# The modulated input's buffer starts at another offset modulo 1024 bytes

## The chip, the core and the metric

The kernel runs on one core of a Trainium2 chip. The metric is the device time of one execution in microseconds; three executions of the kernel before took 1462.16, 1462.6 and 1463.55 us, median 1462.6.

## What is computed

Two groups of 128 tokens (context and latent) pass through a trunk of two layers. Each layer has three sub-layers, and each of these reads its input after a modulation with a scale and a shift:

```python
h = modulate(x, mod[:, :, 0], mod[:, :, 1])                       # x * (1 + scale) + shift
x = layer_norm(ALPHA * x + 0.5 * mod[:, :, 2] * swiglu(h, w_in, w_out), ...)
m, new_ctx = token_mixer(modulate(x, mod[:, :, 3], mod[:, :, 4]), lp, ctx, rope)
x = layer_norm(ALPHA * x + mod[:, :, 5] * m, ...)
h = modulate(x, mod[:, :, 6], mod[:, :, 7])
x = layer_norm(ALPHA * x + 0.5 * mod[:, :, 8] * swiglu(h, w_in2, w_out2), ...)
```

The model width is 1024, the hidden width of a feed-forward block 2816. The mixer projects its input to convolution, retention, attention and gate columns, works on each, and merges them.

## The kernel before, in words

All 256 tokens go through together, as the columns of matmuls; features lie on the 128 partitions. To keep float32 accuracy, weights and activations are each split into a rounded high part and a remainder ("hi" and "lo"). A product is three matmuls of 256 columns: hi weights with hi input, hi weights with lo input, lo weights with hi input (`mmA`). In every one the weights are the stationary operand (128 x 128 numbers, 512 bytes of each partition) and the input is the moving one (256 numbers, 1024 bytes of each partition).

Weights come in units of 512 KB. Each is loaded into `ring_raw` (4 slots), rounded by ScalarE into `ring_hi`, and its remainder is written by VectorE into `ring_lo` (5 slots each), three units ahead of TensorE. A unit of 8 k-tiles is 24 matmuls.

The modulated input of the current sub-layer stands in `ring_U`, 16 KB of each partition: for each of 8 k-tiles its hi part (1024 bytes) and then its lo part. `build_u` fills it once per sub-layer, six times in all. Its readers are these:

- the gate and up projections of a feed-forward block: 44 units, in four blocks;
- the mixer's projections with 256 columns (`proj(ps, self.u)`): 47 units, in two mixers. So 270 units, or 6480 matmuls, read `ring_U` as the moving operand;
- `bunit` in the mixer, the other way round: there a piece of `ring_U` is stationary and 512 columns of the weights move (`mmB`), 384 matmuls in two mixers.

All other products of split numbers read tenant tiles, called T in the profile's rows (or CM): T1, T2, T3, T4, T6, T7 and CM. They hold hidden activations, the normed latents and the merged branches in the same hi/lo layout, and the same `mmA` or `mmB` reads them.

The buffers are laid out one after the other in the order of `RINGS`. In the kernel before, the byte offsets in each partition are these: `ring_raw` 16512, `ring_hi` 32896, `ring_lo` 53376, `ring_ada` 73856, `ring_U` 90240; then the smaller rings and constants; then T4 164800, T2 181184, T3 189376, T1 197568, T6 205760, CM 213952, T7 222144. Modulo 1024, the weight rings and `ring_U` are at 128, and all seven tenant tiles are at 960. Weight k-tiles advance by 512 bytes, so a stationary tile of weights begins at 128 or 640 modulo 1024. The hi and lo parts of an input advance by 1024.

The order of each engine's instructions is set when the program is built, by a list scheduler with its own cost table (`Program.order`). It knows nothing of addresses. L458 is the one matmul call, L480 and L484 are VectorE's calls, L518 is ScalarE's, L463 the four-strip matmuls of the modulation weights.

Of the kernel before, what the change touches and what calls it, by code (L numbers as in the profile page):

```python
# [8 lines left out]
F32 = mybir.dt.float32  # L9
# [7 lines left out]
P = 128  # L17
# [111 lines left out]
def _units():  # L129
    out = []  # L130
    for l in range(L):
        for seq in (_ffn_units(1), _mix_units(), _ffn_units(2)):
            for key, parts in seq:
                out.append((l, key, parts, sum(len(ks) * len(cols) for _, ks, cols in parts)))
    return out
# [93 lines left out]


N_RAW = 4
N_HL = 5
N_ADA = 4
ROUNDS = [0, 0, 8, 8, 8, 0, 8, 0, 0, 8, 8, 2, 8, 8, 8, 4, 8, 2]
# [26 lines left out]
class Op:  # L261
    __slots__ = ("eng", "dur", "fn", "deps", "succ", "late", "due", "chain", "left", "ready", "nbytes", "pad")

    def __init__(self, eng, dur, fn, chain, due, nbytes, pad):
        self.pad = pad
        self.eng, self.dur, self.fn, self.chain, self.due, self.nbytes = eng, dur, fn, chain, due, nbytes
        self.deps, self.succ = set(), []
        self.late, self.left, self.ready = 1e18, 0, 0.0


class Program:
    """Operations in an order that is right, with what each reads and writes; `order` gives every
    engine its own order, by the latest start that keeps the tensor engine's main chain moving."""

    def __init__(self):
        self.ops, self.writes, self.reads = [], {}, {}
# [18 lines left out]
        return name, p0, p0 + dims[0][1], lo, hi  # L295

    def real(self, ap):
        """The access in the kernel's own tile: a tile that shares its memory with earlier ones
        is only made when its first operation is emitted."""
        if not hasattr(ap, "tensor") or ap.tensor.name not in self.tenants:  # L300
            return ap
        name = ap.tensor.name
        tag, _, make = self.tenants[name]
        if name not in self.tiles:
            self.tiles[name] = make()
        x = self.tiles[name]
        if x.dtype != ap.dtype:
            x = x.bitcast(ap.dtype)
        return bass.AP(x.tensor, ap.offset, ap.ap)
# [130 lines left out]


class Recorder:
    """The instructions that the kernel uses, put into a Program."""

    def __init__(self, nc, prog):
        self.nc, self.prog, self.gate = nc, prog, []
# [88 lines left out]


def _ada_plan():
    """(slot, kind, round, index) of every piece of modulation weights in the order of their use:
    kind "k" is a k tile for the tensor engine, "d" transposed columns for the vector engine."""
    f1, m1, f2, l1 = FFN_UNITS, FFN_UNITS + MIX_UNITS, LAYER, LAYER + FFN_UNITS  # L540
    parts = [
        ("k", (0, 1), -1, -1),
        ("d", (2, 3, 4, 5, 8), D0, f1 - 4), ("d", (6, 7), f1 + MIXD_A, f1 + MIXD_B), ("k", (2, 3, 4), 6, f1 - 4), ("k", (5,), f1 - 1, f1 - 1),
        ("k", (6, 7), f1 + MIX_A, f1 + MIX_B), ("k", (8,), m1 - 1, m1 - 1),
        ("d", (9, 10, 11, 12, 13, 14, 15, 17), m1 + 6, l1 - 4), ("d", (16,), l1 + MIXD_A, l1 + MIXD_B), ("k", (9, 10), m1 + 6, f2 - 4), ("k", (11,), f2 - 1, f2 - 1),
        ("k", (12, 13), f2 + 6, l1 - 4), ("k", (14, 15), l1 - 1, l1 - 1),
        ("k", (16,), l1 + MIX_A, l1 + MIX_B), ("k", (17,), l1 + MIX_UNITS - 1, l1 + MIX_UNITS - 1)]
    out = []
    for kind, rounds, a, b in parts:
        seq = [(r, x) for r in rounds for x in range(ROUNDS[r] if kind == "d" else KT - ROUNDS[r])]  # L550
        out += [(a + (b - a) * (i + 0.5) / len(seq), kind, r, x) for i, (r, x) in enumerate(seq)]
    assert len(out) == L * 9 * KT
    return sorted(out, key=lambda e: e[0])
# [9 lines left out]
class Trunk:  # L563
    RINGS = dict(raw=(N_RAW, UNIT), hi=(N_HL, UNIT), lo=(N_HL, UNIT), ada=(N_ADA, 1024), T1=(1, 2048), U=(1, 4096),
                 T2=(1, 2048), T3=(1, 2048), T4=(1, 4096), T6=(1, 2048), T7=(1, 1024), CM=(1, 2048), sg=(8, T),
# [7 lines left out]
    def __init__(self, ctx, tc, io, scratch):  # L573
        self.tc, self.io = tc, io
        self.prog = Program()
        self.nc = Recorder(tc.nc, self.prog)
        self.units = _units()
        self.offs = np.concatenate([[0], np.cumsum([u[3] * P for u in self.units])]).tolist()
        self.keep = ctx.enter_context(tc.tile_pool(name="keep", bufs=1))
        ps = ctx.enter_context(tc.tile_pool(name="ps", bufs=1, space=PSUM))  # L580
        self.rings, self.shared, self.n_tenants = {}, {}, 0
        self.scratch = scratch
        for tag, (n, w) in self.RINGS.items():
            if tag in self.SHARED:
                continue
            x = self.keep.tile([P, n * w], F32, name=f"ring_{tag}")
            self.rings[tag] = [0, [x[:, i * w:(i + 1) * w] for i in range(n)]]
            self.rings[tag].append(x)
        for i in range(4):
            self.rings[f"a{i}"] = [0, [self.rings["aa"][1][i]]]  # L590
        self.banks = {b: ps.tile([P, 512], F32, name=f"bank{b}") for b in self.BANKS}
        self.prog.banks = {b.tensor.name for b in self.banks.values()}
        self.prog.parts = {self.banks["D"].tensor.name}
        self.mmring, self.mmi = ("m0", "m1", "m2", "E"), 0
        self.raw, self.hi, self.lo = {}, {}, {}
        self.cur = 0
        self.n_dma = 0
        self.n_split = 0
        self.stages = {}
        self.bg = []  # L600
        self.bg_rate = 0.0
        self.bg_credit = 0.0
        self.ada_at = 0
        self.ada_t, self.ada_limit = [], 16
        self.plan = _ada_plan()
        self.ada_closing = True
        self.bubbles = [l * LAYER + x - 1 for l in range(L) for x in (FFN_UNITS, FFN_UNITS + MIX_UNITS, LAYER)]
        self.asum, self.half, self.half_done = {}, 0, set()
        self.ada_dma = 0
        self.ada_free = [(x, False) for x in self.rings["ada"][1]]  # L610
# [67 lines left out]
    def ensure_split(self, i):  # L678
        while self.n_split <= min(i, len(self.units) - 1):
# [12 lines left out]
            self.n_split += 1  # L692
            self.ensure_dma(k + N_RAW)

# [180 lines left out]
    def setup(self):  # L875
# [29 lines left out]
        self.ada_flush()  # L905
        self.ensure_dma(N_RAW - 1)
        self.build_u(self.z, A, self.mods(0, 0), lambda f: None)
        self.next_ax(self.z, None)

    def gated(self, fn):  # L910
        """Loads that nothing waits for yet: behind the weights of the next slots."""
        self.nc.gate = [self.lo[max(self.lo)]] if self.lo else []
        fn()
        self.nc.gate = []
# [20 lines left out]
        self.ts(cw, cw, 0.5, None, ALU.mult)  # L935

    def load_rows(self, tag, at, then):
        """SiLU(cond) in every partition, in the memory of `tag`."""
        def load():
            self.rows = self.rings[tag][2].rearrange("p (g n) -> p g n", g=2)  # L940
            self.nc.load(self.rows, self.io["crow"])

        def silu():
            for g in range(2):
                self.act(self.rows[:, g, :], self.rows[:, g, :], AF.Silu)

        assert at <= then
        self.sched(at, lambda: self.gated(load))
        self.sched(then, silu)
# [243 lines left out]
    def mixer(self, l):  # L1193
# [338 lines left out]
        for nh in range(2):  # L1532
            bs = [self.bank() for _ in range(2)]

            def evac_rg(nh=nh):
                if nh == 0:
                    nc.table("silu_and_others")
                for g in range(2):
                    t = self.t("w512", [512])
                    self.act(t, bs[g], AF.Silu)  # L1540
                    oo = ot[:, g, nh * 512:(nh + 1) * 512]
                    self.tt(oo, oo, t, ALU.mult)

            def gated(nh=nh):
                for q in range(2):
                    tp = self.bank("AB"[q])
                    for e in range(2):
                        for g in range(2):
                            c = nh * 512 + (q * 2 + e) * P
                            nc.transpose(tp[:, e * T + g * TOK:e * T + (g + 1) * TOK], ot[:, g, c:c + P], ident)  # L1550
                    ch = catr[:, nh * 4 + q * 2:nh * 4 + q * 2 + 2, 0, :]
                    pv = tp.rearrange("p (e t) -> p e t", e=2)
                    self.act(ch, pv, AF.Copy)
                    self.tt(catr[:, nh * 4 + q * 2:nh * 4 + q * 2 + 2, 1, :], pv, ch.bitcast(F32), ALU.subtract)

            if nh == 0:
                catr = self.t("T4", [KT, 2, T], F32R)
            bunit("rg", nh, bs, evac_rg)
            self.sched(1, gated)
# [265 lines left out]
```

## Time and profile before

| | |
|---|---|
| median of three runs | 1462.6 us |
| profiled execution, first to last instruction | 1456.6 us |
| around the span, against the median | 6.0 us |
| TensorE busy | 1423.0 us, 98% |
| VectorE busy | 1211.3 us, 83% |
| ScalarE busy | 766.5 us, 53% |
| bytes moved, mean rate | 326.60 MB, 224 GB/s |

The page tells each engine's busy time in microseconds and as a share of the span. TensorE's matmuls overlap in the pipeline, so the duration of a single one (some 280 ns) is longer than the time from one to the next. What a matmul costs in a stream is read from the chain of waits, where consecutive matmuls of one bank stand as one piece: its length divided by its count. With 24 matmuls to a unit, 2.88 us a unit is 120 ns a matmul.

### The profile page before, as it was taken

What the parts mean: (1) busy time and instruction counts of PE and PEld (TensorE: products, weight loads), DVE (VectorE), ACT (ScalarE), POOL (GpSimd) and SP (SyncE); (2) the same over time, 40 slices, a digit from 0 to 9 for tenths busy, and PEclk for the clock granted to TensorE, in tenths of its full rate; (3) what the DMA queues carried; (4) which work ended last, traced back from release to release, by engine and by line L of the source; (5) the groups of instructions that cost most, each with busy time, mean ns of one, the idle gap of its engine ahead of it and who ended that gap; (6) DMA issues with size and microseconds to landing.
All of it is one profiled execution on the core that took longest, in us unless ns stands there. A gap on an engine that the chain in (4) does not pass through costs nothing.

```text
span 1456.6 us, 28827 instructions
## 1 busy us (share of the span) xinstructions
PE 1423.0 (98%) x11488; PEld 1358.3 (93%) x11488; DVE 1211.3 (83%) x2291; ACT 766.5 (53%) x1257; POOL 13.6 (1%) x28
## 2 busy tenths in 40 slices
PE   7999999999999999999999999999999999999996
PEld 5999998987999989999989999899788999899996
DVE  3799988988999888999888999789889997855554
ACT  4554447555554566444464444575555455744542
POOL 0000000000100000000000000000000000000000
PEclk9999999999999999999999999999999999999999
DMA  9988875654566767889668886655346767465561
GB/s 342 342 301 272 317 257 208 229 174 123 179 225 224 235 248 241 273 277 327 230 210 276 267 306 204 219 180 158 118 149 192 260 213 244 147 206 183 168 189 55
DMA packets 92166, 326.60 MB, mean 224 GB/s; under 512 B 10944, under 2 KB 11360, under 8 KB 91392
## 3 DMA queue, kind: packets, MB, share of 16 engines
q1 hardware_dynamic: 90432, 319.88, 66.1%
q0 software_dynamic: 1600, 4.88, 1.0%
q8 instruction: 90, 1.47, 0.4%
q14 instruction: 44, 0.36, 0.1%
HBM read 321.28 MB, written 3.44 MB: 223 GB/s over the span
## 4 chain that ended last, share of the span: by engine, by line
PE 92%; DVE 3%; DMA 3%; ACT 1%; issue 0%; SPq 0%; DVEq 0%; ACTq 0%
PE bankm L458 67%; PE bankE L458 18%; PE bankB L458 2%; PE bankA L458 2%; PE bankC L458 2%; DMA T<-in_ada 1%; DVE ring_lo L480 1%; DVE T L484 1%; DVE T L480 1%; DMA T<-in_x 1%; DMA ring_aa<-in_crow 1%; DMA ring_raw<-in_w 0%; DMA ring_ada<-in_ada 0%; PE bankC L471 0%; ACT ring_hi L518 0%
## 5 line engine op out<-in xcount | busy, mean ns | idle before, releaser
L518 ACT ACTIVATE ring_hi<-ring_raw 128x1024 fp32r<-128x1024 f32 (+2 forms) x462 | 476.7, 1036 | 344.1 <-PE bankm L458 154.0
L480 DVE TENSOR_TENSOR ring_lo<-ring_raw,ring_hi 128x1024 fp32r<-128x1024 f32 (+2 forms) x462 | 546.8, 1193 | 95.7 <-ACT ring_hi L518 91.4
L458 PE MATMUL bankm<-ring_U,ring_hi 128*128 128x256 f32 x3296 | 615.5, 286 | 6.1 <-ACT ring_U L518 2.8
L458 PEld LDWEIGHTS bankm<-ring_U,ring_hi 128*128 128x128 f32 x3296 | 517.2, 192 | 13.0 <-ACT ring_U L518 3.8
L458 PE MATMUL bankm<-ring_U,ring_lo 128*128 128x256 f32 x1648 | 473.4, 287 | 0.2
L458 PEld LDWEIGHTS bankm<-ring_U,ring_lo 128*128 128x128 f32 x1648 | 315.6, 191 | 4.0 <-issue 2.3
L458 PE MATMUL bankm<-T,ring_hi 128*128 128x256 f32 x1464 | 263.4, 280 | 1.1 <-DVE T L480 1.1
L458 PEld LDWEIGHTS bankm<-T,ring_hi 128*128 128x128 f32 x1464 | 224.1, 188 | 2.1 <-issue 2.1
L458 PE MATMUL bankm<-T,ring_lo 128*128 128x256 f32 (+1 forms) x732 | 204.7, 280 | 0.0
L458 PE MATMUL bankE<-ring_U,ring_hi 128*128 128x256 f32 x832 | 154.5, 284 | 0.0
L458 PEld LDWEIGHTS bankm<-T,ring_lo 128*128 128x128 f32 x732 | 137.4, 188 | 0.0
L458 PEld LDWEIGHTS bankE<-ring_U,ring_hi 128*128 128x128 f32 x832 | 130.2, 192 | 0.4 <-DVE ring_lo L480 0.4
L458 PE MATMUL bankE<-ring_U,ring_lo 128*128 128x256 f32 x416 | 118.1, 284 | 0.0
L484 DVE SCALAR_TENSOR_TENSOR T<-hp,cols,T 128x256 f32<-128x256 f32 x240 | 114.2, 481 | 3.8
L518 ACT ACTIVATE ring_tB<-bankm 128x256 f32<-128x256 f32 x84 | 31.8, 384 | 117.8 <-PE bankm L458 117.8
L458 PE MATMUL bankE<-T,ring_hi 128*128 128x256 f32 (+1 forms) x488 | 88.9, 281 | 0.0
L458 PE MATMUL bankm<-ring_hi,ring_U 128*128 128x512 f32 x256 | 88.2, 412 | 0.0
L458 PEld LDWEIGHTS bankE<-ring_U,ring_lo 128*128 128x128 f32 x416 | 79.9, 192 | 0.3 <-DVE ring_lo L480 0.3
L484 DVE SCALAR_TENSOR_TENSOR ring_s<-ring_ada,ring_sg 128x1024 bf16<-128x1024 f32 (+2 forms) x68 | 74.4, 1094 | 2.0 <-DMA ring_ada<-in_ada 1.8
L458 PEld LDWEIGHTS bankE<-T,ring_hi 128*128 128x128 f32 x488 | 74.9, 188 | 1.0 <-DVE T L480 0.8
L484 DVE SCALAR_TENSOR_TENSOR ring_ada<-ring_ada,ring_sg 128x1024 f32<-128x1024 f32 (+2 forms) x68 | 73.9, 1093 | 0.1
L458 PE MATMUL bankE<-T,ring_lo 128*128 128x256 f32 (+1 forms) x244 | 68.7, 281 | 0.0
(263 smaller groups left out, 1598.2 us busy)
## 6 DMA issues: line engine op xcount, KB each, us to landing
ring_raw<-in_w SPq DMA_DIRECT2D x422, 512.0 KB, 4.4
ring_ada<-in_ada SPq DMA_DIRECT2D x107, 512.0 KB, 4.9
ring_raw<-in_w SPq DMA_DIRECT2D x32, 384.0 KB, 4.1
T<-in_ada SPq DMA_DIRECT2D x17, 512.0 KB, 7.0
ring_aa<-in_ada SPq DMA_DIRECT2D x10, 512.0 KB, 5.8
CM<-in_ada SPq DMA_DIRECT2D x6, 512.0 KB, 6.3
ring_sg<-in_crow SPq DMA_DIRECT2D x3, 1024.0 KB, 6.0
ring_raw<-in_w SPq DMA_DIRECT2D x8, 256.0 KB, 7.5
```

The lines of the kernel that those rows point to most:

```text
L458: self.prog.add("PE", dur, lambda: self.nc.tensor.matmul(self.real(out), self.real(lhsT), self.real(rhs), start=start, stop=stop), [lhsT, ...
L480: self.dve(out, [in0, in1], lambda: self.nc.vector.tensor_tensor(out=self.real(out), in0=self.real(in0), in1=self.real(in1), op=op))
L484: self.dve(out, [in0, scalar, in1], lambda: self.nc.vector.scalar_tensor_tensor(out=self.real(out), in0=self.real(in0), scalar=self.real(s ...
L518: self.prog.add("ACT", dur, lambda: self.nc.scalar.activation(self.real(out), self.real(in_), func, **{k: self.real(v) for k, v in kw.item ...
```

## The change

An unused tile of 208 float32 numbers (832 bytes of each partition) is put ahead of `ring_U`, and one of 48 numbers (192 bytes) behind it. `ring_U` moves from 90240 to 91072, that is from 128 to 960 modulo 1024. Every buffer behind it moves by 832 + 192 = 1024 bytes, so its offset modulo 1024 stays; `ring_raw`, `ring_hi`, `ring_lo` and `ring_ada` don't move. Every engine has the same instructions in the same order with the same waits; only addresses differ. The other lines of the diff take out six one- and two-line descriptions of functions and classes.

```diff
+U_LEAD = 208
...
         for tag, (n, w) in self.RINGS.items():
             if tag in self.SHARED:
                 continue
+            if tag == "U":
+                self.keep.tile([P, U_LEAD], F32, name="lead_u")
             x = self.keep.tile([P, n * w], F32, name=f"ring_{tag}")
+            if tag == "U":
+                self.keep.tile([P, 256 - U_LEAD], F32, name="tail_u")
             self.rings[tag] = [0, [x[:, i * w:(i + 1) * w] for i in range(n)]]
```

## Rows read from the trace of the kernel before

**Rows 1.** Span and mean granted clock of the core
```profile
core 0: 1456.6 us, clock 0.994
```
**Rows 2.** The page: busy time of the engines, and the granted clock in 40 slices
```profile
PE 1423.0 (98%) x11488; PEld 1358.3 (93%) x11488; DVE 1211.3 (83%) x2291; ACT 766.5 (53%) x1257; POOL 13.6 (1%) x28
...
PEclk9999999999999999999999999999999999999999
```
**Rows 3.** The page: the chain that ended last, shares of the span by engine
```profile
PE 92%; DVE 3%; DMA 3%; ACT 1%; issue 0%; SPq 0%; DVEq 0%; ACTq 0%
```
**Rows 4.** Waits of TensorE: waiter, releaser: us in total, times, longest
```profile
PE bankD L463 <- DMA T<-in_ada: 7.8, 6, 5.4
...
PE bankm L458 <- ACT ring_U L518: 2.8, 4, 1.7
```
**Rows 5.** Groups of matmuls by shape: tiles (out<-operands), count | busy us, mean ns | idle
```profile
L458 PE MATMUL bankm<-ring_U,ring_hi 128*128 128x256 f32 x3296 | 615.5, 286 | 6.1 <-ACT ring_U L518 2.8 <-ACT ring_hi L518 2.6 <-DVE ring_U L480 0.3
L458 PE MATMUL bankm<-ring_U,ring_lo 128*128 128x256 f32 x1648 | 473.4, 287 | 0.2
L458 PE MATMUL bankm<-T,ring_hi 128*128 128x256 f32 x1440 | 257.1, 279 | 0.0
...
L458 PE MATMUL bankm<-ring_hi,ring_U 128*128 128x512 f32 x256 | 88.2, 412 | 0.0
...
L458 PE MATMUL bankm<-ring_lo,ring_U 128*128 128x512 f32 x128 | 53.9, 421 | 0.0
...
L458 PE MATMUL bankm<-ring_hi,T 128*128 128x512 f32 x24 | 7.8, 395 | 0.0
```
**Rows 6.** The chain in order of time: start us, length us, engine, bank, matmuls
```profile
146.36 2.88 PE bankE L458 x24
...
170.54 18.37 PE bankm L458 x156
...
443.50 2.83 PE bankE L458 x24
...
455.34 2.88 PE bankE L458 x24
...
662.88 2.88 PE bankE L458 x24
...
686.49 18.13 PE bankm L458 x160
...
882.40 18.61 PE bankm L458 x158
...
1395.36 18.49 PE bankm L458 x157
```
**Rows 7.** The same chain: 384-column matmuls, then 512-column ones of T, of ring_U
```profile
288.48 1.04 PE bankE L458 x6
289.53 4.20 PE bankm L458 x18
...
396.46 6.13 PE bankm L458 x27
```
**Rows 8.** Stretches: us, busy us (count) of PE, PEld, DVE, ACT, POOL; clock, DMA
```profile
40.00:150.00 110.00, 110.00 (x919) 110.00 (x918) 97.82 (x152) 57.14 (x84) 0.00 (x0) 1.00 0.88 301
156.00:188.00 32.00, 32.00 (x274) 32.00 (x273) 28.47 (x45) 12.14 (x14) 0.00 (x0) 1.00 0.91 338
560.00:670.00 110.00, 110.00 (x919) 110.00 (x918) 100.96 (x166) 54.85 (x80) 0.00 (x0) 1.00 0.83 270
672.00:703.00 31.00, 31.00 (x276) 31.00 (x276) 29.75 (x54) 12.74 (x14) 0.00 (x0) 1.00 0.90 320
```
**Rows 9.** The attention stretches of both mixers, instructions that touch ring_U alone
```profile
285.00:424.00 139.00, 111.70 (x591) 86.26 (x592) 0.00 (x0) 0.00 (x0) 1.00 0.53 174
985.00:1130.00 145.00, 109.88 (x576) 84.37 (x576) 0.00 (x0) 0.00 (x0) 1.00 0.50 155
```

## The prediction

> **What bounds the kernel now.** I read the page first: TensorE is busy for 1423.0 us of a span of 1456.6 us, and the granted clock is full but for moments, 0.994 in the mean, the upper of its two levels, 2.4 GHz [rows 1, 2]. The chain that ended last is 92% TensorE [rows 3], and TensorE waits little: the largest item of its list of waits is 7.8 us, for modulation weights at the start, and it waited 2.8 us for ring_U itself [rows 4]. So nearly the whole span is one stream of matmuls, and time can only go if a matmul takes less. The change moves no instruction, no wait and no transfer. Only an effect of the address on a matmul's own pace can change the time, so I looked at the pace.
>
> **The pace.** In the chain, a unit of 24 matmuls that read ring_U takes 2.88 us, 120.0 ns each: in the first feed-forward block, in the mixer, and in layer 0's second block (at 146.36, 455.34 and 662.88 us) [rows 6]. 256 columns at 2.4 GHz are 106.7 ns, so 13.3 ns of each are something else. The matmuls on T tiles have the same shape, come from the same function and use the same weight rings, and they are faster: 18.37 us for 156 is 117.76 ns, 18.61 for 158 and 18.49 for 157 are 117.8, and in one stretch, the output projection of layer 0's second block, 18.13 for 160 is 113.31 [rows 6]. The grouped durations agree: 286 and 287 ns a matmul for ring_U, 279 for T [rows 5].
>
> Is that the operand or the stage? In the mixer, units on U and on T alternate, with one set of neighbours, one scheduler and the same work on the other engines: there a unit on CM takes 2.83 us and one on U, 12 us later, 2.88 [rows 6]. So it goes with the operand, and what differs in the operand is its address: ring_U begins at 128 modulo 1024, as the weight rings do, and all seven tenant tiles at 960. They lie between 164800 and 226240 and are equally fast wherever they lie there. After the change ring_U is at 960 too.
>
> **The sum, part by part.** The two padding tiles are never written or read: nothing. The shift by 1024 of the buffers behind: nothing, because a period over 1024 would have to tell the T reads that begin at 960 modulo 2048 from those at 1984 (the hi and lo parts of one tile alternate between the two), and the 113.31 stretch holds both at one pace. Writing ring_U (48 instructions on each of two engines) I leave at nothing.
>
> What is left are the matmuls that read ring_U.
>
> - 6480 with 256 columns (270 units of 24). I take it that they get T's pace. T has two paces, 117.76 and 113.31, so the price is bounded by 2.24 and 6.69 ns each, and by nothing if the address is not the cause. Which pace a stream has seems to be set where it starts or is broken: the output projection begins straight behind the U units with no wait between, and ran at the slower pace in three blocks of four and at the faster one in layer 0's second block. I take each block's U units to be in the mode in which its T units follow.
> - Of the 6480, the attention stretches of both mixers hold 783 (591 and 576 instructions, less 192 each that are the 512-column kind) [rows 9]. There the stream is broken every few matmuls by attention's own, and TensorE is on U for only 111.70 of 139 us. Price between 0 and 783 x 2.24 = 1.8 us; I take the middle, 0.9.
> - The other 5697 at 2.24 ns: 12.8 us.
> - Layer 0's second block, 44 units or 1056 matmuls, at the faster pace: a further 117.76 - 113.31 = 4.45 ns each, 4.7 us.
> - 384 with 512 columns, where ring_U is the stationary operand (x256 and x128) [rows 5]. Here the row speaks against the change: with U's tiles at 128 and 640, 27 of them take 6.13 us, 227.0 ns; with T's at 960 and 448, 18 take 4.20 us, 233.3 ns [rows 7]. After the change they have the offsets of T: a loss of 0 to 384 x 6.3 = 2.4 us. Since these stretches too are broken up, I take 1.2 us.
>
> Sum: -12.8 - 0.9 - 4.7 + 1.2 = -17.2 us. The span goes from 1456.6 to 1439.4. The median is 6.0 us above the span, so 1445.4 us, 1.2% less.
>
> **What could be late next.** VectorE. In 40 to 150 us it is busy 97.82 of 110 us, in 560 to 670 us 100.96 [rows 8]. At 117.76 ns the same work stands in 107.9 us, 91% and 94%; at 113.31 in 103.9 us, 94% and 97%. In the fast T stretch it already runs 29.75 of 31 us, 96%, at 320 GB/s of loads, and TensorE is busy all through [rows 8]. So it gives a limit to the fast pace, not to the slower one.
>
> A rule that speaks against all this: the Trainium skill, page "SBUF — State Buffer", section "Who interferes with whom", says that only the port pair shared by VectorE and GpSimd causes contention, that TensorE has two read ports of its own for the moving operand and the weights, and that it never waits on anyone. The page "TensorE: Matmul & The Clock Gate", section "Back-to-back issue gap", makes the gap a matter of the column count alone. By the two, U and T would have one pace and the change would give 1462.6 us. The chain's 120.0 against 117.8 and 113.3 ns at one column count does not agree with that, though it doesn't show that the offset is the reason.
>
> **Rivals.**
>
> - *All in the fast mode.* 6480 x 6.69 = 43.3 us less: 1419.3 us. For it: the mode exists and held for over 31 us on end [rows 8]. Against: three output projections of four ran in the slower one, and VectorE would be at 94 to 97%.
> - *The offset is not the cause*, and U is slower for where it lies: at 90 KB with the weight rings below it at 33 to 74 KB, while all T tiles lie above 160 KB. A shift of 832 bytes does nothing then: 1462.6 us. For it: no row has a T tile at 128, or a 256-column operand in the lower part at 960; and the 384-column matmuls of T take 1.04 us for 6, or 173.3 ns [rows 7], which is 13.3 over 160.0 and so no better than U's. Against: with 512 columns it is U that has the faster pairs, though it lies beside the weights.
> - *Unequal offsets cost, and T is fast for another reason.* In the one pair of rows with the two operands' places exchanged, equal offsets modulo 512 (128 and 128) take 227.0 ns and unequal ones 233.3 [rows 7]. If inequality is what costs and height is what helps T, the change puts 6.3 ns on 6480 matmuls: 40.8 us, 1503 us. Its place is the gate and up units, and it decides as soon as a unit takes over 2.88 us. Against: T's 256-column reads are unequal to the weights in the same way and are fast.
>
> **How the numbers follow.** T's pace with about today's mix of modes, 1434 to 1457 us: 0.58. Mostly fast mode, 1419 to 1434: 0.17. No effect: 0.13. Slower: 0.12. A difference of 0.2%, 2.9 us, is about what a measurement of this kernel can tell from none. So faster 0.75, same 0.13, slower 0.12. The likeliest case gives 1445.4. The range goes from the all-fast bound, 1421, to no effect, 1463, and leaves out the slower case and the edge of the all-fast one.
>
> **What would show it.** Right: U units in the chain take 2.83 us (slower mode) or 2.72 (faster mode) for 24 instead of 2.88, T units stay at 117.8 or 113.3, the 512-column pieces on U go from 227 to 233 ns, and the mean of U's groups falls from 286 ns to about 280. Wrong: U still at 2.88 us, which makes the operand's height or another thing the cause; or U faster and TensorE idle before ring_lo, which makes VectorE the bound and gives part back.

## The result and the profile after

The changed kernel takes 1447.76 us in the median (1441.44 to 1451.04), against 1462.38 us: a ratio of 0.9899, 95% interval 0.988 to 0.9919. A second set of executions beside another set of before gave 1447.58 and 1460.45 us, ratio 0.9906, 0.9887 to 0.9924. So 13 to 15 us went, where 17 were forecast.

The rows that answer to [rows 1] and [rows 5], of the changed kernel (its lines are one higher than those of before, L458 is L459):

```profile
core 0: 1449.3 us, clock 0.992
```
```profile
L459 PE MATMUL bankm<-ring_U,ring_hi 128*128 128x256 f32 x3296 | 607.6, 283 | 6.7 <-ACT ring_hi L519 3.0 <-ACT ring_U L519 3.0 <-DVE ring_U L481 0.3
L459 PE MATMUL bankm<-ring_U,ring_lo 128*128 128x256 f32 x1648 | 469.0, 285 | 0.2
L459 PE MATMUL bankm<-T,ring_hi 128*128 128x256 f32 x1440 | 257.9, 280 | 0.0
L459 PE MATMUL bankm<-ring_hi,ring_U 128*128 128x512 f32 x256 | 88.8, 414 | 0.0
```

The mean of ring_U's matmuls fell from 286 to 283 ns and from 287 to 285; T's rose from 279 to 280; the 512-column ones on ring_U rose from 412 to 414. These means mix stages: in 40 to 150 us, inside the first block, the first of these groups went from 283 to 280 ns, and in 285 to 424 us, the attention stretch, from 294 to 292. The pace stands in the chain of the changed kernel, which answers to [rows 6, 7] (start, length, engine, bank, matmuls):

```profile
144.31 2.83 PE bankE L459 x24
...
168.33 18.38 PE bankm L459 x156
...
289.00 4.20 PE bankm L459 x18
...
395.73 6.30 PE bankm L459 x27
...
442.49 2.83 PE bankE L459 x24
...
454.23 2.83 PE bankE L459 x24
...
659.28 2.83 PE bankE L459 x24
...
675.53 7.77 PE bankE L459 x66
```

A unit on ring_U now takes 2.83 us, 117.9 ns a matmul, in the first block, in the mixer and in layer 0's second block; in the mixer the units on CM and on ring_U (442.49, 454.23) have become equal. The 512-column piece on ring_U went from 6.13 to 6.30 us for 27, that is to the 233.3 ns of T's pieces. And one stretch got slower: the output projection behind layer 0's second block, at 113.3 ns before, is now at 7.77 / 66 = 117.7.

Between the sub-layers TensorE waits, and there its granted clock can fall. The windows round four of these joins, of the changed kernel (us; then PE, PEld, DVE, ACT, POOL busy; clock, DMA share, GB/s):

```profile
222.00:237.00 15.00, 12.81 (x99) 12.43 (x100) 9.39 (x29) 8.86 (x23) 0.54 (x1) 0.89 0.49 184
734.00:749.00 15.00, 13.41 (x109) 12.27 (x100) 13.97 (x43) 11.20 (x26) 0.00 (x0) 0.89 0.49 168
923.00:938.00 15.00, 12.54 (x114) 10.72 (x113) 13.36 (x37) 11.48 (x29) 0.54 (x1) 1.00 0.81 291
1240.00:1255.00 15.00, 13.00 (x114) 11.18 (x113) 13.54 (x41) 13.22 (x33) 0.00 (x0) 0.89 0.22 70
```

In three of the four the granted clock is at 0.89 in the mean, a dip to the lower level, 1.2 GHz, for a part of the window. In the profiled execution of before, only the third join had one:

```profile
222.00:237.00 15.00, 12.99 (x125) 11.83 (x118) 11.60 (x38) 10.75 (x27) 0.54 (x1) 1.00 0.57 219
734.00:749.00 15.00, 13.40 (x132) 11.38 (x131) 15.00 (x44) 12.93 (x34) 0.00 (x0) 1.00 0.54 177
930.00:945.00 15.00, 12.54 (x102) 10.80 (x101) 13.45 (x41) 12.52 (x34) 0.54 (x1) 0.89 0.68 233
1250.00:1265.00 15.00, 12.96 (x107) 12.44 (x104) 11.67 (x36) 12.57 (x30) 0.00 (x0) 1.00 0.27 100
```

This comes up again with the last experiments.

### The profile page after: what moved, and what is told of

The parts are those of the page before. It is cut to its first block, busy times and chain, and to the rows that moved or that the text cites. A ratio compares the mean times of both kernels' runs of the same rounds, so it can differ in the third digit from the quotient of the medians.

```text
span 1449.3 us, 28827 instructions
## 1 busy us (share of the span) xinstructions
PE 1415.5 (98%) x11488; PEld 1349.7 (93%) x11488; DVE 1211.5 (84%) x2291; ACT 766.3 (53%) x1257; POOL 13.6 (1%) x28
## 4 chain that ended last, share of the span: by engine, by line
PE 94%; DVE 2%; DMA 2%; ACT 1%; issue 0%; SPq 0%; DVEq 0%; ACTq 0%
PE bankm L459 68%; PE bankE L459 19%; PE bankB L459 2%; PE bankA L459 2%; PE bankC L459 2%; DMA T<-in_ada 1%; DMA T<-in_x 1%; DVE T L481 1%; DVE T L485 1%; DMA ring_ada<-in_ada 0%; PE bankC L472 0%; PE bankD L464 0%; DVE ring_lo L481 0%; DVE ring_w L481 0%; ACT ring_hi L519 0%
## 5 line engine op out<-in xcount | busy, mean ns | idle before, releaser
L459 PE MATMUL bankm<-ring_U,ring_hi 128*128 128x256 f32 x3296 | 607.6, 283 | 6.7 <-ACT ring_hi L519 3.0
L459 PEld LDWEIGHTS bankm<-ring_U,ring_hi 128*128 128x128 f32 x3296 | 510.1, 189 | 13.5 <-ACT ring_U L519 4.2
L459 PE MATMUL bankm<-ring_U,ring_lo 128*128 128x256 f32 x1648 | 469.0, 285 | 0.2
L459 PEld LDWEIGHTS bankm<-ring_U,ring_lo 128*128 128x128 f32 x1648 | 311.1, 189 | 4.0 <-issue 2.3
L459 PE MATMUL bankm<-T,ring_hi 128*128 128x256 f32 x1464 | 264.2, 281 | 0.9 <-DVE T L481 0.9
L459 PEld LDWEIGHTS bankm<-T,ring_hi 128*128 128x128 f32 x1464 | 224.2, 188 | 1.9 <-issue 1.9
L459 PE MATMUL bankm<-T,ring_lo 128*128 128x256 f32 (+1 forms) x732 | 205.1, 280 | 0.0
L459 PE MATMUL bankE<-ring_U,ring_hi 128*128 128x256 f32 x832 | 152.2, 281 | 0.0
L459 PEld LDWEIGHTS bankm<-T,ring_lo 128*128 128x128 f32 x732 | 137.1, 187 | 0.0
L459 PEld LDWEIGHTS bankE<-ring_U,ring_hi 128*128 128x128 f32 x832 | 128.1, 189 | 0.4 <-DVE ring_lo L481 0.4
L459 PE MATMUL bankE<-ring_U,ring_lo 128*128 128x256 f32 x416 | 116.8, 281 | 0.1
L459 PE MATMUL bankE<-T,ring_hi 128*128 128x256 f32 (+1 forms) x488 | 89.2, 282 | 0.0
L459 PE MATMUL bankm<-ring_hi,ring_U 128*128 128x512 f32 x256 | 88.8, 414 | 0.0
L459 PEld LDWEIGHTS bankE<-ring_U,ring_lo 128*128 128x128 f32 x416 | 78.4, 188 | 0.3 <-DVE ring_lo L481 0.3
L459 PEld LDWEIGHTS bankE<-T,ring_hi 128*128 128x128 f32 x488 | 75.0, 188 | 1.0 <-DVE T L481 0.8
L459 PE MATMUL bankE<-T,ring_lo 128*128 128x256 f32 (+1 forms) x244 | 68.8, 282 | 0.0
```

Of the source, the lines that this page charges most:

```text
L459: self.prog.add("PE", dur, lambda: self.nc.tensor.matmul(self.real(out), self.real(lhsT), self.real(rhs), start=start, stop=stop), [lhsT, ...
```

## The experiments

The theory: the pace of a stream of split matmuls depends on the distance between the starts of its two operands, the moving one and the stationary one. Rivals: the place in memory, high or low (the padding as such); the moving operand's own offset, whatever the weights'; equality modulo 512 as the only bad case. All edits below are against the kernel before. "Distance" is the start of the moving operand less that of the weights.

### Moved, but at the same offset

```diff
+            if tag == "U":
+                self.keep.tile([P, 256], F32, name="lead_u")
             x = self.keep.tile([P, n * w], F32, name=f"ring_{tag}")
```

> All 1024 bytes of padding stand ahead of ring_U, none behind: ring_U at 91264, 192 bytes above its place in the changed kernel, but again at 128 modulo 1024. The offset theories (pace set by the start modulo 1024 or less) expect the pace of before: 2.88 us a unit of ring_U, 120.0 ns a matmul, 227 ns with 512 columns, about 1462 us. The rival of the place (higher is faster, or padding itself helps) expects the pace of the changed kernel: 2.83 us a unit and about 1448 us.

Measured: 1460.91 us beside 1461.35, ratio 0.9992, interval 0.9982 to 1.0002. Its chain:

```profile
100.23 2.88 PE bankE L458 x24
...
170.50 18.37 PE bankm L458 x156
...
688.69 18.84 PE bankm L458 x160
```

The pace of before. Neither the higher place nor padding does anything; the offset does. T, too, keeps its 117.8 ns when it moves by 1024 bytes. The last row is the T stretch behind layer 0's second block, which took 18.13 us in the profile of before [rows 6]: with the same offsets modulo 1024 it is now at 18.84 / 160 = 117.8 ns.

### The weights moved, the input left

```diff
+            if tag == "hi":
+                self.keep.tile([P, 208], F32, name="lead_w")
             x = self.keep.tile([P, n * w], F32, name=f"ring_{tag}")
+            if tag == "lo":
+                self.keep.tile([P, 48], F32, name="tail_w")
```

> ring_hi and ring_lo start at 960 modulo 1024 in place of 128 (k tiles at 960 and 448); ring_U stays at 128 and the T tiles at 960. Theory A, that the distance between the moving and the stationary operand counts: T is now at distance 0 (or 512) and slows from 117.8 to 120.0 ns, that is 2.88 us for 24, while ring_U, at distance 192 modulo 512, leaves 120.0 for 117.8 or 113.3. Theory B, that the moving operand's own offset counts: ring_U stays at 120.0 ns, T at 117.8 or 113.3, and the time at 1462 us. With 512 columns on ring_U, A expects 233 ns, B 227.

Measured: 1434.82 us (1428.81 to 1443.49), ratio 0.9823, interval 0.9782 to 0.9863. The profiled execution is the shortest of the four. Its chain, with units on ring_U at both ends, two pieces on T and a 512-column piece:

```profile
96.61 2.72 PE bankE L458 x24
...
156.19 7.92 PE bankE L458 x66
164.11 18.72 PE bankm L458 x156
...
390.04 6.19 PE bankm L458 x27
...
572.31 2.72 PE bankE L458 x24
```

T, whose tiles kept their offset, went from 117.8 to 120.0 ns (7.92 / 66, 18.72 / 156). ring_U, which kept its own, went from 120.0 to 113.3 (2.72 / 24), in all four blocks of this execution; the longer ones weren't profiled. So it is the pair that counts and not the operand's own offset. The 512-column pieces took 229.3 ns (6.19 / 27), which neither theory had.

### A map of the distances

Six kernels put ring_U and the T tiles at other offsets, with two numbers each: the lead and tail round ring_U, and a lead ahead of the T tiles.

```diff
+                self.keep.tile([P, LEAD], F32, name="lead_u")
             x = self.keep.tile([P, n * w], F32, name=f"ring_{tag}")
+                self.keep.tile([P, 256 - LEAD], F32, name="tail_u")
...
         self.hp = self.keep.tile([P, 4, 2, PADW], F32, name="hp")
+        self.keep.tile([P, LEAD_T], F32, name="lead_t")
```

LEAD 80, LEAD_T 64:

> ring_U at 448 and the T tiles at 192 modulo 1024, weights at 128 and 640 as before. If the period is 512 bytes, ring_U at 448 is the same as at 960: 117.8 ns (or 113.3 in the fast mode), 2.83 us a unit, 233 ns with 512 columns. If it is 1024 or more, ring_U may have another pace. T at 192 is 64 bytes off the weights: if only exact equality costs, T keeps 117.8 or 113.3; if it is a matter of degree, it lies between 117.8 and 120.0.

LEAD 128, LEAD_T 80:

> ring_U at 640 and the T tiles at 256 modulo 1024, weights at 128 and 640 as before. Period 512: ring_U keeps 120.0 ns, 2.88 us a unit, 227 ns with 512 columns. Period 1024: ring_U at a distance of 512 from half of the weight tiles and 0 from the others, as before, so only its own offset could change its pace. T at 256 is 128 bytes off the weights: 117.8 or 113.3 if only near equality costs.

LEAD 64, LEAD_T 144:

> Weights at 128 and 640, ring_U at 384 (distance 256 modulo 512), T at 512 (distance 384). A map of the distances not yet seen. If only distance 0 is bad: both at 117.8 or 113.3 ns. If the half distance of 256 is bad as well: ring_U at 118.5 to 120.0.

LEAD 112, LEAD_T 104:

> Weights at 128 and 640, ring_U at 576 (distance 448), T at 352 (distance 224). If the grain is 64 bytes or more, T at 224 has the pace of 192 (113.3 ns) or of 256; ring_U at 448, which is 64 below equality, 117.8 or 113.3 ns if only equality costs.

LEAD 40, LEAD_T 72:

> Weights at 128 and 640, ring_U at 288, T at 224: distances 160 and 96 modulo 256, no multiples of 64. With the grain of 64 bytes that the run with T at 352 (distance 224, 118.2 to 118.8 ns) suggests, both lie at 118 to 119 ns and neither reaches 113.3. If the pace is a smooth function of the distance, 160 lies between 118.8 (distance 128) and 113.3 (distance 192), 96 between 117.8 and 118.8.

LEAD 8, LEAD_T 96:

> Weights at 128 and 640, ring_U at 160 (distance 32), T at 320 (distance 192). Distance 32, half a grain from equality: 120.0 ns if a collision of the same 64 bytes is what costs, 118 to 119 if any offset off the grain costs the same. T at 192: 113.3 or 117.8 ns, as in the run with all at 320.

Rows of their chains. Input at 448, T at 192:

```profile
96.60 2.72 PE bankE L458 x24
...
163.24 17.68 PE bankm L458 x156
...
387.64 6.30 PE bankm L458 x27
...
572.04 2.83 PE bankE L458 x24
```
Input at 640, T at 256:
```profile
100.44 2.88 PE bankE L458 x24
...
170.83 18.51 PE bankm L458 x156
```
Input at 384, T at 512:
```profile
99.68 2.88 PE bankE L458 x24
...
170.06 18.51 PE bankm L458 x156
```
Input at 576, T at 352:
```profile
97.28 2.72 PE bankE L458 x24
...
164.57 18.46 PE bankm L458 x156
```
Input at 288, T at 224:
```profile
99.17 2.82 PE bankE L458 x24
...
168.50 18.71 PE bankm L458 x156
...
767.55 2.85 PE bankE L458 x24
```
Input at 160, T at 320:
```profile
98.32 2.80 PE bankE L458 x24
...
166.49 17.68 PE bankm L458 x156
```

In one table, with the runs before it. The pace is length by count; where two are given, stretches of one run had one or the other.

| distance mod 256 | seen as (modulo 1024) | ns a matmul of 256 columns |
|---|---|---|
| 0 | input 128, 640 and 384 with weights 128; T 960 with weights 960 | 120.0 |
| 32 | input 160 | 116.7 |
| 64 | T 960 and 192, input 960 and 448 | 117.8 or 113.3 |
| 96 | T 224 | 119.9 |
| 128 | T 256 and 512 | 118.7 |
| 160 | input 288 | 117.5 or 118.8 |
| 192 | input 576; input 128 with weights 960; T 320 | 113.3 or 117.8 |
| 224 | T 352 | 118.3 |

The input at 384 is 256 bytes from the weights and as slow as at equality, so the period is 256 bytes and not the 512 of the theory. T at 256 and at 512 have one distance modulo 256 and one pace; the input at 448 has the 117.8 ns of the input at 960, but 113.3 in its first block. The distances 32, 96, 160 and 224 rest on one pair of places each. Equality is not the only bad case: 96 bytes cost the same. The wish for a smooth curve and that for a grain of 64 bytes both fail at 32 and 96 bytes. Each of the six ran once, and their times follow the paces: 1444.2 us (input 448), 1430.6 (576) and 1436.5 (160) beside some 1461, but 1466.5 and 1462.7 for the two that left the input at 120.0 ns and slowed T to 118.7, and 1462.0 where T went to 119.9.

### Everything at a distance of 192

With LEAD 48 and LEAD_T 96 the input and T stand at 320:

> ring_U and all T tiles at 320 modulo 1024, weights at 128 and 640: every 256-column pair is at distance 192 modulo 512, the one at which ring_U ran at 113.3 ns throughout with the weights at 960. If the distance alone sets the pace: ring_U and T both at 113.3 ns, 2.72 us a unit; against 1461.4 us that is 5697 x 6.7 = 38 us, half of 783 x 6.7 = 3 us, and for 3456 T matmuls from mostly 117.8 to 113.3 some 14 us less, 1 us back from the 512-column pairs: about 1408 us, or up to 1415 if VectorE falls behind. If instead the absolute places mattered in that run (a moving start that is a multiple of 128), 320 is no such multiple: 117.8 ns, about 1448 us.

With the weights at 960 as above and LEAD_T 48 the input and T stand at 128:

> Weight rings at 960 and 448, ring_U and all T tiles at 128: distance 192 modulo 512 for all again, at other absolute places than with everything at 320. If the distance alone counts: the same paces, 113.3 ns for ring_U and T, and the same time within 5 us, about 1408 us.

Measured: 1426.05 us, ratio 0.9738 (0.9709 to 0.9768), and 1421.23 us, ratio 0.9714 (0.9687 to 0.9741). Both are well ahead of the changed kernel, and both miss the 1408 us that was expected. The second one's chain, first in the first block, then in the mixer, then in layer 0's second block:

```profile
96.67 2.72 PE bankE L458 x24
...
163.30 17.68 PE bankm L458 x156
...
423.58 8.48 PE bankm L458 x72
...
469.64 8.16 PE bankm L458 x72
...
567.31 2.83 PE bankE L458 x24
...
670.48 18.85 PE bankm L458 x160
```

The first block runs at 113.3 ns, input and T; the second at 117.9. So the distance of 192 permits the fast mode but does not force it. In the mixer, units on the input and on T follow each other without a break, and both have one pace, first 117.8 ns (8.48 / 72) and later 113.3 (8.16 / 72). This suggests that a stream keeps the pace of what ran just before it; by what rule the pace changes, these runs don't settle. VectorE was not what held the slower blocks back: in the fast first block TensorE is busy throughout, with VectorE at 98.03 of 105 us:

```profile
40.00:145.00 105.00, 105.00 (x928) 105.00 (x928) 98.03 (x155) 57.81 (x84) 0.00 (x0) 1.00 0.91 317
```

### The changed kernel and the fastest once more

The changed kernel, with the descriptions of its functions left in:

```diff
+                self.keep.tile([P, 208], F32, name="lead_u")
             x = self.keep.tile([P, n * w], F32, name=f"ring_{tag}")
+                self.keep.tile([P, 48], F32, name="tail_u")
```

> The changed kernel once more (ring_U at 960, the descriptions left in), to see what spreads its executions over 10 us where the kernel before has 3 to 6. Theory of the modes: a stream that starts in the fast mode runs at 113.3 ns until it is broken, so an execution with one feed-forward block in the fast mode is 1056 x 4.45 = 4.7 us (with its output projection up to 7 us) shorter; the profile shows at least one block at 113.3 where its time is under 1446 us, and none where it is over 1449. Rival: only the clock's dips between the sub-layers differ (1 to 2.4 us each), and every block is at 117.8. Median 1447 us.

And the second of the two layouts above, with no edit to it:

> The fastest layout so far once more (weights at 960, ring_U and T at 128, distance 192 throughout), beside the changed kernel on one chip. If the distance theory holds it is faster than the changed kernel by 20 to 35 us, 1415 to 1427 us, and its executions differ by the modes of their blocks.

Measured: 1447.58 us (1442.28 to 1450.21) and 1421.56 us (1419.53 to 1424.48; ratio 0.9732, 0.9716 to 0.9748). The profiled execution of the changed kernel took 1447.57 us, between the two bounds that were set, and had every block at 117.9 ns:

```profile
99.90 2.83 PE bankE L458 x24
...
169.15 18.37 PE bankm L458 x156
...
566.90 2.83 PE bankE L458 x24
```

It spans 1445.8 us, 3.5 less than the first profile of the same layout, at the same paces. Of its four joins only one has a dip, the one that had it in the kernel before:

```profile
222.00:237.00 15.00, 13.12 (x115) 12.74 (x116) 11.06 (x32) 11.51 (x29) 0.54 (x1) 1.00 0.52 200
734.00:749.00 15.00, 14.23 (x116) 13.79 (x117) 13.95 (x38) 12.32 (x30) 0.00 (x0) 1.00 0.41 144
923.00:938.00 15.00, 12.54 (x103) 10.77 (x102) 13.71 (x42) 12.79 (x34) 0.54 (x1) 0.89 0.68 236
1240.00:1255.00 15.00, 12.96 (x124) 11.62 (x117) 12.50 (x38) 12.68 (x31) 0.00 (x0) 1.00 0.26 79
```

So the first profile's two dips more go with a span 3.5 us longer, although its first block began 0.8 us earlier (39.72 us against 40.54), and dips explain a part of the spread. They don't explain all of it: the execution of 1441.44 us has a mean granted clock of 0.996, as the profiled one of 1447.57 us has, and is 6.1 us shorter. By the sum in the expectation, a block in the fast mode would be 4.7 to 7 us. Whether the shortest executions (1441.44, 1442.28) had one is open: neither was profiled.

The fastest layout came out 26.0 us ahead of the changed kernel, as expected. Its second profile has layer 0's second block in the other mode than its first (2.83 us at 567.31):

```profile
568.58 2.72 PE bankE L458 x24
```

The last block changed the other way, from 2.72 to 2.83 us a unit. So one layout had the fast mode in different blocks in two executions.

## Why the prediction was right, and where it was not

- *The cause.* Right: a program with the same instructions in the same order lost 1% because the matmuls on ring_U went from 120.0 to some 117.8 ns, T's pace. The argument from the mixer, where T and input units alternate, carried it. The rival of the place fell with the first experiment. That of unequal offsets, in the form given, fell with the result: units went to 2.83 us. That of the fast mode in all blocks did not come about: no block of either profile had it. The stated range of 1421 to 1463 us held no change as well, so what confirms the cause is the unit's 2.83 us and the two experiments, not that the time lies in the range.
- *The slower-mode price.* Right. The cleanest pair of spans is the second profile of the changed layout, 1445.8 us, and that of before, 1456.6, each with one dip at the same join: 10.8 us. In between, before had a T stretch of some 33 us in the fast mode, worth 293 x 4.45 ns = 1.3 us, and the changed one had not. So the input's matmuls gave back 12.1 us, or 12.8 if one allows for a first block that began 0.7 us later (40.54 against 39.80), where the terms 12.8 + 0.9 - 1.2 make 12.5. How the 0.9 and the 1.2, two middles of a range, came out one by one is not shown.
- *The 512-column loss.* Right in sign and in the pace, 227.0 to 233.3 ns a matmul.
- *The grouped durations.* The mean of ring_U's groups was to fall to about 280 ns and fell to 283 and 285. The 7 ns between ring_U's groups and T's were not all pace: the mean of ring_U's takes in the attention stretches, at 294 ns before and 292 after. Within a block it did fall to 280.
- *The fast mode of layer 0's second block.* This step failed: 4.7 us were taken off for it. The T stretch behind that block did run at 113.31 ns before [rows 6], but in the changed layout the block, and the stretch, ran at 117.8 in both profiled executions. The mode was read as a property of the block, and it goes with the execution: with the offsets of before, the first experiment's profile has that T stretch at 117.8 ns, and the fastest layout's two profiles have different blocks in the fast mode. Without this term the forecast is 12.5 us less, 1450.1 us; the two medians are 1447.76 and 1447.58, which is 14.6 and 12.9 us less than before. The sum without the term lies nearer to both.
- *The step from span to median.* The 6.0 us were taken as time around the span. The executions that list both have 1.7 to 1.8 us around it (1451.04 and 1449.3 in the changed kernel). So the profiled execution of before was itself some 4 us shorter than the median.
- *VectorE as the next bound.* It wasn't, here or in the block at 113.3 ns.
- *The rule that spoke against it.* The Trainium skill, page "SBUF — State Buffer", section "Who interferes with whom", gives TensorE two independent read ports and says that it never waits on anyone. No run here shows another engine slowing it. But moving the weights alone changed the pace of input and T in opposite directions (120.0 to 113.3 and 117.8 to 120.0 ns), so for TensorE's own two operands the starts matter, and here the measurement decides. Whether one of the two reads waits for the other, and which, the trace doesn't show.

## What to carry to other kernels

Where TensorE is the bound, compare the pace of matmuls of one shape on different buffers: a few ns between them, seen within one stage, can be the distance of the two operands' starts, and padding in front of a buffer changes it for nothing. Move the operand that all streams share (here the weights), or all the others together, and map the distances instead of copying the one buffer that looks good: 960 was worth 1%, and 128 with the weights at 960 nearly 3%. Look at both roles of a buffer, since the distance that helps it as the moving operand may cost it as the stationary one.

## What was not expected of the hardware

- The period is 256 bytes: the input at 128, 384 and 640 with the weights at 128 and 640 had 120.0 ns in all four blocks.
- Equality is the slowest case for 256 columns (120.0 ns, beside 119.9 at 96 bytes) and the fastest seen for 512 (227.0, against 229.3 and 233.3).
- At distances of 64 and 192 a stream has two paces, 117.8 and 113.3 ns, and keeps one over hundreds of matmuls; in the chains read here it changed where other matmuls came between or the operands changed. At a distance of 160 it has two as well, 117.5 and 118.8 ns.
